# Attention of a two-layer trunk: one pipeline over all groups of tokens and heads, and the largest scores of a head gathered by one product and a DMA

## The chip, the core and the metric

The kernel runs on one core of one Trainium2 chip. A core has five engines with queues of their own: TensorE (PE, whose weight loads are listed apart as PEld), VectorE (DVE), ScalarE (ACT), GpSimd (POOL) and SyncE (SP, which here issues most of the DMAs). PE writes its products into PSUM, from where DVE or ACT take them. The metric is the device time of one execution in microseconds (us). The kernel before took 3489.2 us, the median of 3 runs (3480.62 to 3492.08).

## The reference

A trunk of two layers over 1024 latent tokens and 256 context tokens, with 1024 features. Each layer mixes the tokens in four ways (an mLSTM, an attention, an SSD and an S5 mixer, 256 features each), projects the four results out and then runs a gated feed-forward net. Only the attention is touched:

```python
q = jnp.concatenate([q_nope, q_rope], axis=-1)      # 4 heads, 64 + 32 features
k = jnp.concatenate([k_nope, jnp.broadcast_to(kr, k_nope.shape[:-1] + (MLA_ROPE,))], axis=-1)

def attend(q, k, v):
    s = jnp.einsum('bqhd,bkhd->bhqk', q, k).astype(jnp.float32) * scale
    p = jax.nn.softmax(s, axis=-1).astype(v.dtype)
    return jnp.einsum('bhqk,bkhd->bqhd', p, v)

yc = attend(qc, kc, vc)              # context tokens see the context alone
yl = attend(ql, k_all, v_all)        # latent tokens see all 1280
```

## The kernel before

Tokens lie along the free axis, in ten chunks of 128: chunks 0 and 1 are the context, 2 to 9 the latents. Queries are worked on in groups of columns: (0,256) for the context, (256,512) and (768,512) for the latents. Layer 0 has all three groups and ten chunks; the last layer drops the context's queries and has two groups and eight chunks. To keep single-precision accuracy, queries and keys are each held as a high part (`qh`, `kh`) and a small remainder (`ql`, `kl`), and a product of scores is three matmuls: high by high, high by low, low by high (L1020 to L1022).

**Largest scores.** `scores(h)` (L952) makes the keys of head h, and then the largest score of each query, so that the exponent stays in range. For each chunk of 128 queries it makes one to three products `a_pm` (L970), chunk by 512 or 256 keys, of the high parts alone; DVE reduces each to one column of `a_mx` (L971), and a second small reduce (L972) joins the columns of a chunk. For each group, one product per chunk with that single column as weights and the identity as data (`a_pmr`, L975) lays the chunk's 128 maxima into one row of PSUM, on partition 96; ACT copies the row, negated, into row 96 of `qh` (L976). Row 96 of `kh` holds ones, so the first matmul of a score product, over 97 rows (L1020), subtracts the maximum by itself. A single-precision product of this kind stands in the trace as two matmuls, so 72 products `a_pmr` are 144 records.

**Attention.** `attend` (L978) goes over two pairs of heads, and in each over the heads, the groups and steps of two key chunks (`k0` = 0, 2, ... 8; the context group has one step). One step is six matmuls into `a_pst`, a tile of two PSUM banks of which there is only one; an exponential on ACT into `a_E` (L1024, three buffers); the two value products into `a_po` (L1014, one bank) of the step before; and two sums of the exponentials over the keys into `a_S`, one on POOL and one on DVE (L1033). A group's last value products come right after its last step, then ACT and DVE move `a_po` out (L1036, L1037). `finish` (L1039) closes a group of a pair of heads: a sum on DVE, two products with ones that add `a_S` over the partitions (`a_pr`, L1044), the reciprocal (L1045), the product on POOL (L1046) and the DMA of the result to `YD`. It is put off to a later step by the list `later`; before the pair's next use, `a_S` (one buffer for each group) has to be read by it.

**What sets the order.** `scores(h + 1)` is written before head h's groups, and between groups `extra()` puts in cells of the mLSTM and pieces of the modulation (`wm` loads of 512 KB, products `pm1_...`, L172 and L183) by a fixed table. The program is then ordered on each engine by a list scheduler at build time, which goes by data, buffers and priorities; `TOGETHER` raises that of the value products and of `a_pr`. In this stretch `K.acc` hands out just two PSUM banks in turn (pool `pd`), and key products, `a_pm`, `a_pmr` and `a_pr` all take them in the order in which the program is written. `a_pr` of head 1 is written after all of `scores(3)`, and takes its bank after it.

## Time and profile before

| | us |
|---|---|
| median of 3 runs | 3489.2 (3480.62 to 3492.08) |
| the profiled execution | 3488.96 |
| its span in the profile | 3487.1 |
| PE busy | 3223.8 (92% of the span) |
| DVE busy | 2133.4 (61%) |
| ACT busy | 1217.1 (35%) |
| POOL busy | 1180.6 (34%) |

The profile is of one execution: every instruction of each engine with its start, its duration and what ended the idle time ahead of it. Times inside it count from the span's start. The attention of layer 0 lies from 567 to 864 us, that of layer 1 from 2410 to 2663 us. Busy times of a long stretch say little on what a short one waits for; the stretch itself has to be looked at.

### The profile page before, as it was taken

What the parts mean: (1) busy time and instruction counts of PE and PEld (TensorE: products, weight loads), DVE (VectorE), ACT (ScalarE), POOL (GpSimd) and SP (SyncE); (2) the same over time, 40 slices, a digit from 0 to 9 for tenths busy, and PEclk for the clock granted to TensorE, in tenths of its full rate; (3) what the DMA queues carried; (4) which work ended last, traced back from release to release, by engine and by line L of the source; (5) the groups of instructions that cost most, each with busy time, mean ns of one, the idle gap of its engine ahead of it and who ended that gap; (6) DMA issues with size and microseconds to landing.
All of it is one profiled execution on the core that took longest, in us unless ns stands there. A gap on an engine that the chain in (4) does not pass through costs nothing.

```text
span 3487.1 us, 47319 instructions
## 1 busy us (share of the span) xinstructions
PE 3223.8 (92%) x17678; PEld 2655.9 (76%) x17678; DVE 2133.4 (61%) x4065; ACT 1217.1 (35%) x2025; POOL 1180.6 (34%) x1109
## 2 busy tenths in 40 slices
PE   7899997997989999998999899997988899999996
PEld 6898895554778888886788789995645788887785
DVE  7857648675485343439778583536855855555654
ACT  4223534332244333333211424533323444444211
POOL 1912424223146444442211021323323376554120
PEclk9999997998999999999999999998989999999998
DMA  5677534254322121225332465534152322223321
GB/s 203 168 205 216 161 113 144 92 188 146 133 67 85 65 73 66 73 78 187 116 103 84 126 209 167 154 115 128 53 208 97 103 91 80 83 89 136 127 78 49
DMA packets 287157, 423.51 MB, mean 121 GB/s; under 512 B 91016, under 2 KB 197200, under 8 KB 286928
## 3 DMA queue, kind: packets, MB, share of 16 engines
q1 hardware_dynamic: 176788, 301.29, 27.5%
q10 hardware_dynamic: 110140, 119.20, 10.3%
q8 instruction: 139, 2.28, 0.3%
q14 instruction: 90, 0.74, 0.1%
HBM read 301.48 MB, written 118.91 MB: 121 GB/s over the span
## 4 chain that ended last, share of the span: by engine, by line
PE 38%; DVE 8%; DMA 3%; ACT 2%; issue 2%; POOL 0%; SPq 0%; ACTq 0%; DVEq 0%; POOLq 0%
PE pd L313 4%; PE pd L314 4%; PE pd L312 4%; PE px L312 2%; PE px L314 2%; PE px L313 2%; PE ps_in L312 1%; PE ps_in L314 1%; PE ps_in L313 1%; PE a_po L1014 1%; PE pz L312 1%; PE pz L313 1%; PE pz L314 1%; PE ps_out L312 1%; PE ps_out L313 1%
## 5 line engine op out<-in xcount | busy, mean ns | idle before, releaser
L313 PE MATMUL pd<-fl,wh_d 128*128 128x512 f32 (+1 forms) x896 | 334.0, 376 | 16.3 <-DVE fl L230 16.3
L312 PE MATMUL pd<-fh,wh_d 128*128 128x512 f32 (+1 forms) x896 | 328.6, 377 | 21.4 <-ACT fh L229 10.1
L314 PE MATMUL pd<-fh,wl_d 128*128 128x512 f32 (+1 forms) x896 | 329.6, 373 | 0.0
L230 POOL TENSOR_TENSOR wl_d<-wr_d,wh_d 128x1024 fp32r<-128x1024 f32 x44 | 110.7, 2534 | 472.5 <-ACT wh_d L229 472.4
L1709 DVE SCALAR_TENSOR_TENSOR xx<-pd,modv,xx 128x512 f32<-128x512 f32 (+1 forms) x248 | 165.3, 678 | 122.8 <-PE pd L314 122.0
L312 PE MATMUL ps_in<-ha,wh_in 128*128 128x384 f32 (+3 forms) x688 | 216.7, 325 | 11.8 <-ACT st L1533 11.3
L314 PE MATMUL ps_in<-ha,wl_in 128*128 128x384 f32 (+3 forms) x688 | 222.0, 323 | 0.0
L313 PE MATMUL ps_in<-ha,wh_in 128*128 128x384 f32 (+3 forms) x688 | 221.9, 323 | 0.0
L312 PE MATMUL ps_in<-hc,wh_in 128*128 128x256 f32 (+1 forms) x704 | 214.6, 307 | 7.3 <-ACT hc L244 4.6
L312 PEld LDWEIGHTS pd<-fh,wh_d 128*128 128x128 f32 x896 | 172.1, 193 | 57.5 <-ACT fh L229 12.8
L313 PE MATMUL ps_in<-hc,wh_in 128*128 128x256 f32 (+1 forms) x704 | 214.0, 305 | 0.7 <-DVE hc L245 0.7
L314 PE MATMUL ps_in<-hc,wl_in 128*128 128x256 f32 (+1 forms) x704 | 213.2, 303 | 0.0
L313 PEld LDWEIGHTS pd<-fl,wh_d 128*128 128x128 f32 x896 | 173.0, 194 | 48.3 <-DVE fl L230 21.0
L314 PEld LDWEIGHTS pd<-fh,wl_d 128*128 128x128 f32 x896 | 172.9, 193 | 28.3
L230 POOL TENSOR_TENSOR wlo_u<-wr_u,whi_u 128x1024 fp32r<-128x1024 f32 x44 | 106.0, 2410 | 215.9 <-ACT whi_u L229 194.6
L971 DVE TENSOR_REDUCE a_mx<-a_pm 128x1 f32<-128x512 f32 (+1 forms) x200 | 112.8, 589 | 61.5 <-PE a_pm L970 60.2
L1024 ACT ACTIVATE a_E<-a_pst 128x1024 f32<-128x1024 f32 (+1 forms) x84 | 84.3, 1003 | 186.7 <-PE a_pst L1022 165.7
L229 ACT CAST wh_d<-wr_d 128x1024 fp32r<-128x1024 f32 x44 | 45.2, 1048 | 298.1 <-PE pd L313 213.8
L230 DVE TENSOR_TENSOR wlo_s<-wr_s,whi_s 128x1024 fp32r<-128x1024 f32 x42 | 71.1, 1694 | 119.9 <-ACT whi_s L229 119.9
L312 PEld LDWEIGHTS ps_in<-ha,wh_in 128*128 128x128 f32 x688 | 132.3, 193 | 14.7 <-ACT st L1533 12.0
L312 PEld LDWEIGHTS ps_in<-hc,wh_in 128*128 128x128 f32 x704 | 134.9, 192 | 9.7 <-ACT hc L244 5.6
L313 PEld LDWEIGHTS ps_in<-hc,wh_in 128*128 128x128 f32 x704 | 135.3, 192 | 2.6 <-DVE hc L245 1.9
(647 smaller groups left out, 9496.9 us busy)
## 6 DMA issues: line engine op xcount, KB each, us to landing
wm<-in_w_mod SPq DMA_DIRECT2D x96, 512.0 KB
wr_in<-in_w_in SPq DMA_DIRECT2D x44, 512.0 KB
wr_u<-in_w_up SPq DMA_DIRECT2D x44, 512.0 KB
wr_g<-in_w_up SPq DMA_DIRECT2D x44, 512.0 KB
wr_d<-in_w_down SPq DMA_DIRECT2D x44, 512.0 KB
wr_out<-in_w_out SPq DMA_DIRECT2D x32, 512.0 KB
HD<-u ACTq DMA_DIRECT2D x22, 640.0 KB
hr<-HD SPq DMA_DIRECT2D x22, 640.0 KB
```

Source lines behind the costliest of these rows:

```text
L229: nc.scalar.copy(hi, src)
L230: (eng or nc.gpsimd).tensor_tensor(lo, src, hi.bitcast(F32), OP.subtract)
L312: mm(ps, whi(k), ahi(k), start=start and i == 0, stop=False)
L313: mm(ps, whi(k), alo(k), start=False, stop=False)
L314: mm(ps, wlo(k), ahi(k), start=False, stop=stop and i == len(ks) - 1)
L971: nc.vector.tensor_reduce(mx[:, c, j:j + 1], ps[:, :kw], mybir.AxisListType.X, OP.max)
L1014: nc.tensor.matmul(po[64 * i:64 * i + 64, :w], vt[:, k0 + i, h], E[:, i, :w], start=k0 == 0, stop=k0 + 2 == nk)
L1024: nc.scalar.activation(E[:, :, :w], ps[:, :, :w], AF.Exp, scale=scale)
L1709: nc.vector.scalar_tensor_tensor(v, ps, K.modv[l][:, 8 * part + m, c:c + 1], v, OP.mult, OP.add)
```

## The change

The change rewrites the second half of `scores` and the loop of `attend`.

In `scores`, the largest scores of a chunk stay apart in `mx` (three columns) and are joined for all latent chunks of a head by one reduce into `mf`. One product per head, with the head's 8 or 10 columns of `mf` as weights, lays them as 8 or 10 rows of 128; ACT copies these, negated, into the small tile `row`, and a DMA on SP's queue writes them one behind the other into row 96 of `qh`. The product for each chunk and the copies for each group go.

In `attend`, `old` is carried over groups and heads: the last value products of a group, and moving `po` out, are written inside the first step of the next group. `S` has three parts in place of four: the sum of the pair's first head is joined at once into `S[:, 2]`, so that the second head can use the first two again. `finish` reads `S[:, 2]` and `S[:, 0]`, and what has been put off is done at `k0 == 4`, or in the context's single step.

```diff
@@ -960,20 +960,22 @@
                         lambda k: self.kvh[:, 0, t0:t0 + w], lambda k: self.kvl[:, 0, t0:t0 + w], 1)
             nc.scalar.copy(kh[:64, t0:t0 + w], ps[:64, :w])
             nc.vector.tensor_tensor(kl[:64, t0:t0 + w], ps[:64, :w], kh[:64, t0:t0 + w].bitcast(F32), OP.subtract)
-        mx = pool.tile([P, NCH, 4], F32, tag="mx", name=n(f"mx{h}"), bufs=2)
-        for t0, w in self.groups:
-            cs = range(t0 // P, (t0 + w) // P)
-            for c in cs:
-                ks = [(0, 256)] if c < 2 else [(0, 512), (512, 512), (1024, 256)]
-                for j, (k0, kw) in enumerate(ks):
-                    ps = K.acc(n(f"pm{h}{c}{j}"))
-                    nc.tensor.matmul(ps[:, :kw], qh[:96, c * P:c * P + P], kh[:96, k0:k0 + kw], start=True, stop=True)
-                    nc.vector.tensor_reduce(mx[:, c, j:j + 1], ps[:, :kw], mybir.AxisListType.X, OP.max)
-                nc.vector.tensor_reduce(mx[:, c, 3:4], mx[:, c, :len(ks)], mybir.AxisListType.X, OP.max)
-            ps = K.acc(n(f"pmr{h}{t0}"))
-            for i, c in enumerate(cs):
-                nc.tensor.matmul(ps[96:97, i * P:i * P + P], mx[:, c, 3:4], K.ident, start=i == 0, stop=i == len(cs) - 1, skip_group_check=True)
-            nc.scalar.activation(qh[96:97, t0:t0 + w], ps[96:97, :w], AF.Copy, scale=-1.0)
+        mx = pool.tile([P, NCH, 3], F32, tag="mx", name=n(f"mx{h}"), bufs=2)
+        mf = pool.tile([P, NCH], F32, tag="mf", name=n(f"mf{h}"), bufs=2)
+        c0, m = self.groups[0][0] // P, len(self.oc)
+        for c in oc:
+            ks = [(0, 256)] if c < 2 else [(0, 512), (512, 512), (1024, 256)]
+            for j, (k0, kw) in enumerate(ks):
+                ps = K.acc(n(f"pm{h}{c}{j}"))
+                nc.tensor.matmul(ps[:, :kw], qh[:96, c * P:c * P + P], kh[:96, k0:k0 + kw], start=True, stop=True)
+                nc.vector.tensor_reduce(mf[:, c:c + 1] if c < 2 else mx[:, c, j:j + 1], ps[:, :kw], mybir.AxisListType.X, OP.max)
+        nc.vector.tensor_reduce(mf[:, 2:], mx[:, 2:], mybir.AxisListType.X, OP.max)
+
+        ps = K.acc(n(f"pmr{h}"))
+        nc.tensor.matmul(ps[:m, :P], mf[:, c0:], K.ident, start=True, stop=True)
+        row = pool.tile([NCH, P], F32R, tag="mr", name=n(f"mr{h}"), bufs=2)
+        nc.scalar.activation(row[:m], ps[:m, :P], AF.Copy, scale=-1.0)
+        nc.sync.dma_start(qh.bitcast(F32)[96:97, c0 * P:].rearrange("o (c t) -> o c t", t=P), row.bitcast(F32)[:m])
 
     def attend(self, pool, epool, y_put, extra):
 
@@ -989,30 +991,44 @@
             while later:
                 later.pop(0)()
 
+        def values(po, h, w, nk, k0, E):
+            with K.tc.high_priority(TOGETHER):
+                for i in range(2):
+                    nc.tensor.matmul(po[64 * i:64 * i + 64, :w], vt[:, k0 + i, h], E[:, i, :w], start=k0 == 0, stop=k0 + 2 == nk)
+
+        def finish(h, t0, w, y, r, S):
+            ps = K.acc(n(f"pr{h}{t0}"))
+            nc.vector.tensor_tensor(S[:, 0], S[:, 0], S[:, 1], OP.add)
+            with K.tc.high_priority(TOGETHER):
+                for i in range(2):
+                    nc.tensor.matmul(ps[64 * i:64 * i + 64, :w], K.ones[:, :64], S[:, 2 - 2 * i], start=True, stop=True)
+            nc.vector.reciprocal(r, ps[:, :w])
+            nc.gpsimd.tensor_tensor(y, y, r, OP.mult)
+            y_put(2 + h // 2, 1, y[:, None, :w], t0, w)
+
+        def evac(po, h, w, y, r):
+            me, ot = slice(64 * (h % 2), 64 * (h % 2) + 64), slice(64 - 64 * (h % 2), 128 - 64 * (h % 2))
+            nc.scalar.copy(r[me, :w], po[ot, :w])
+            nc.vector.tensor_tensor(y[me, :w], po[me, :w], r[me, :w], OP.add)
+
+
         self.scores(0, pool)
+        old, ends = None, []
         for hp in range(2):
             ys = {}
             for ho in range(2):
                 h = 2 * hp + ho
                 kh, kl, qh, ql = self.kh[ho], self.kl[ho], self.qh[h], self.ql[h]
-                me, ot = slice(64 * ho, 64 * ho + 64), slice(64 - 64 * ho, 128 - 64 * ho)
                 if h < 3:
                     self.scores(h + 1, pool)
                 for t0, w in groups:
                     extra()
                     if not ho:
                         ys[t0] = [pool.tile([P, w], F32, tag=f"a{i}{t0}", name=n(f"{i}{hp}{t0}")) for i in "yr"]
-                        ys[t0].append(epool.tile([P, 2, 2, w], F32, tag=f"S{t0}", name=n(f"S{hp}{t0}"), bufs=1))
+                        ys[t0].append(epool.tile([P, 3, w], F32, tag=f"S{t0}", name=n(f"S{hp}{t0}"), bufs=1))
                     y, r, S = ys[t0]
-                    po = K.pa.tile([P, 512], F32, tag="m", name=n(f"po{h}{t0}"))
                     nk = 2 if t0 < TC else NCH
-                    old = None
-
-                    def values(k0, E):
-                        with K.tc.high_priority(TOGETHER):
-                          for i in range(2):
-                            nc.tensor.matmul(po[64 * i:64 * i + 64, :w], vt[:, k0 + i, h], E[:, i, :w], start=k0 == 0, stop=k0 + 2 == nk)
-
+                    po = None
                     for k0 in range(0, nk, 2):
                         ps = K.pa.tile([P, 2, 512], F32, tag="s", name=n(f"pst{h}{t0}{k0}"))
                         for i in range(2):
@@ -1024,32 +1040,25 @@
                         nc.scalar.activation(E[:, :, :w], ps[:, :, :w], AF.Exp, scale=scale)
                         if old:
                             values(*old)
-                        if k0 == 2:
-                            settle()
+                            if not k0:
+                                ends.pop(0)()
                         for i in range(2):
                             if nk == 2:
-                                eng[i].tensor_copy(S[:, i, ho], E[:, i, :w])
+                                eng[i].tensor_copy(S[:, i], E[:, i, :w])
                             elif k0:
-                                eng[i].tensor_tensor(S[:, i, ho], old[1][:, i, :w] if k0 == 2 else S[:, i, ho], E[:, i, :w], OP.add)
-                        old = k0, E
-                    values(*old)
-                    nc.scalar.copy(r[me, :w], po[ot, :w])
-                    nc.vector.tensor_tensor(y[me, :w], po[me, :w], r[me, :w], OP.add)
-
-                    def finish(h=h, t0=t0, w=w, y=y, r=r, S=S, hp=hp):
-                        ps = K.acc(n(f"pr{h}{t0}"))
-                        nc.vector.tensor_tensor(S[:, 0], S[:, 0], S[:, 1], OP.add)
-                        with K.tc.high_priority(TOGETHER):
-                          for i in range(2):
-                            nc.tensor.matmul(ps[64 * i:64 * i + 64, :w], K.ones[:, :64], S[:, 0, i], start=True, stop=True)
-                        nc.vector.reciprocal(r, ps[:, :w])
-                        nc.gpsimd.tensor_tensor(y, y, r, OP.mult)
-                        y_put(2 + hp, 1, y[:, None, :w], t0, w)
-
-                    settle()
-                    if ho:
-                        later.append(finish)
+                                eng[i].tensor_tensor(S[:, i], old[5][:, i, :w] if k0 == 2 else S[:, i], E[:, i, :w], OP.add)
+                        if k0 == 4 or nk == 2:
+                            settle()
+                        po = po or K.pa.tile([P, 512], F32, tag="m", name=n(f"po{h}{t0}"))
+                        old = po, h, w, nk, k0, E
+                    ends.append(functools.partial(evac, po, h, w, y, r))
+                    if not ho:
+                        nc.vector.tensor_tensor(S[:, 2], S[:, 0], S[:, 1], OP.add)
+                    else:
+                        later.append(functools.partial(finish, h, t0, w, y, r, S))
                     extra()
+        values(*old)
+        ends.pop(0)()
         settle()
```

Since a scheduler sets the order, the code alone doesn't show where the instructions come to stand. Three places follow, in layer 0, with the order that the build gives.

PE, at the end of the products for head 3's maxima (`a0_pm3..`, two digits of chunk and part behind the head), before: `a0_pr1768` is the sum over partitions for head 1, group 768, `a0_pst27688` the scores of head 2, group 768, step 8, `a0_po2768` its value products, and `pm1_..` modulation.

```order
L970 MATMUL a0_pm380_8453<-a0_kh1_6517,a0_qh3_6600 128x512
L970 MATMUL a0_pm381_8456<-a0_kh1_6517,a0_qh3_6600 128x512
L970 MATMUL a0_pm382_8459<-a0_kh1_6517,a0_qh3_6600 128x256
L970 MATMUL a0_pm390_8463<-a0_kh1_6517,a0_qh3_6600 128x512
L970 MATMUL a0_pm391_8466<-a0_kh1_6517,a0_qh3_6600 128x512
L970 MATMUL a0_pm392_8469<-a0_kh1_6517,a0_qh3_6600 128x256
L975 MATMUL a0_pmr3768_8473<-cst_60,a0_mx3_8374 1x128 x3
L1044 MATMUL a0_pr1768_8498<-a0_S0768_7638,ones_68 64x512 x2
L975 MATMUL a0_pmr3768_8473<-cst_60,a0_mx3_8374 1x128
L172 MATMUL pm1_12_8750<-wm1_12_8745,sc_84 32x512 x8
L1014 MATMUL a0_po2768_8662<-a0_E27686_8705,a0_vt_6520 64x512 x2
L1020 MATMUL a0_pst27688_8711<-a0_qh2_6599,a0_kh0_6516 128x512
```

After, the same place:

```order
L970 MATMUL a0_pm391_8390<-a0_kh1_6517,a0_qh3_6600 128x512
L172 MATMUL pm1_0_8542<-wm1_0_8467,sc_84 32x512 x8
L970 MATMUL a0_pm392_8393<-a0_kh1_6517,a0_qh3_6600 128x256
L183 MATMUL pm1_0_8542<-msel_82,wms1_0_8551 128x2 x4
L975 MATMUL a0_pmr3_8397<-cst_60,a0_mf3_8317 10x128
L1004 MATMUL a0_pr1768_8420<-a0_S0768_7598,ones_68 64x512 x2
L1004 MATMUL a0_pr30_8749<-a0_S10_8404,ones_68 64x256
L172 MATMUL pm1_4_8563<-wm1_4_8558,sc_84 32x512 x8
L183 MATMUL pm1_4_8563<-msel_82,wms1_4_8572 128x2 x4
L1004 MATMUL a0_pr3256_8822<-a0_S1256_8474,ones_68 64x512
L997 MATMUL a0_po2768_8600<-a0_E27686_8634,a0_vt_6520 64x512 x2
L1036 MATMUL a0_pst27688_8640<-a0_qh2_6599,a0_kh0_6516 128x512
```

`a0_pr1768` still comes behind the last product for head 3's maxima, and the first of the two matmuls of the next sums (`a0_pr30`, `a0_pr3256`), which read `S[:, 2]`, now stand here too. Between the last matmul but one of the step ahead (`a0_pst27686`) and `a0_pr1768` there stood 16 products `a0_pm3..` before, and there stand 7 now; in layer 1 it is 14 and 5.

SP, from the loads of modulation weights to the first input tiles of the stage behind the attention, before:

```order
L156 DMA wm1_4_8633<-in_w_mod 128x1024 x4
L156 DMA wm1_8_8654<-in_w_mod 128x1024 x4
L1736 DMA yraw0_4_0_9001<-YD_100 128x256
L1736 DMA yraw0_4_256_9005<-YD_100 128x512
L1736 DMA yraw0_4_768_9009<-YD_100 128x512
L1736 DMA yraw0_5_0_9013<-YD_100 128x256
L1740 DMA x00_8997<-in_x 128x8x256
L1740 DMA x0256_8993<-in_x 128x8x512
L299 DMA wr_out0_0_256_9100<-in_w_out 128x1024
L156 DMA wm1_12_8745<-in_w_mod 128x1024 x4
```

After:

```order
L156 DMA wm1_4_8558<-in_w_mod 128x1024 x4
L156 DMA wm1_8_8579<-in_w_mod 128x1024 x4
L978 DMA a0_qh3_6600<-a0_mr3_8399 1x10x128
L1745 DMA yraw0_4_0_8931<-YD_100 128x256
L1745 DMA yraw0_4_256_8935<-YD_100 128x512
L1745 DMA yraw0_4_768_8939<-YD_100 128x512
L1745 DMA yraw0_5_0_8943<-YD_100 128x256
L156 DMA wm1_12_8671<-in_w_mod 128x1024 x4
```

The DMA that writes head 3's row into `qh` comes to stand right behind the eight loads `wm1_4` and `wm1_8`, and ahead of the first loads of `yraw`.

ACT, before: `a0_E37688` is the last exponential of head 3, `hb...` are casts of the mixers' results for the projection behind the attention.

```order
L1024 ACTIVATE a0_E37688_8919<-a0_pst37688_8912 128x1024
L1036 COPY a0_r1768_8660<-a0_po3768_8856 64x512
L229 CAST hb004_8961<-yraw0_4_0_9001 128x256
L229 CAST hb004_8961<-yraw0_4_256_9005 128x512
L229 CAST hb004_8961<-yraw0_4_768_9009 128x512
L229 CAST hb005_8963<-yraw0_5_0_9013 128x256
L229 CAST hb005_8963<-yraw0_5_256_9017 128x512
```

After, eleven exponentials ahead of the last one: `a0_E27688` is the last of head 2, `a0_E300` the first of head 3.

```order
L1040 ACTIVATE a0_E27688_8647<-a0_pst27688_8640 128x1024
L229 CAST hb004_8891<-yraw0_4_0_8931 128x256
L229 CAST hb004_8891<-yraw0_4_256_8935 128x512
L229 CAST hb004_8891<-yraw0_4_768_8939 128x512
L229 CAST hb005_8893<-yraw0_5_0_8943 128x256
L181 COPY wms1_8_8663<-pm1_8_8654 128x512
L1011 COPY a0_r1768_8585<-a0_po2768_8600 64x512
L1040 ACTIVATE a0_E300_8700<-a0_pst300_8693 128x2x256
```

The casts stood behind all exponentials; now the first four of the 24 stand between those of heads 2 and 3, and eight more further on between the exponentials of head 3. The projection's first products, some 35 of them, have moved into the same stretch on PE.

## Rows read from the trace of the kernel before

**Rows 1.** The page: span and count of instructions.
```profile
span 3487.1 us, 47319 instructions
```
**Rows 2.** Busy time by stretch: us, then PE, PEld, DVE, ACT, POOL, PEclk, DMA share, GB/s.
```profile
586.00:785.00 199.00, 195.20 (x1066) 118.64 (x1067) 141.24 (x330) 69.68 (x103) 48.61 (x45) 0.95 0.39 133
785.00:809.00 24.00, 19.54 (x90) 9.17 (x89) 15.93 (x29) 4.32 (x6) 3.58 (x3) 0.79 0.78 279
...
2429.00:2585.00 156.00, 153.51 (x830) 91.29 (x831) 112.01 (x243) 54.02 (x76) 43.82 (x37) 0.99 0.40 142
2585.00:2606.00 21.00, 13.32 (x40) 5.62 (x38) 15.12 (x24) 2.92 (x4) 3.78 (x3) 0.72 0.25 86
```
**Rows 3.** Timeline 776:812, layer 0: start, us, engine line op, shapes [idle before <-releaser].
```profile
780.52 1.02 ACT L1024 ACTIVATE a_E<-a_pst 128x1024 f32<-128x1024 f32 x1 [2.02 <-PE a_pst L1022]
...
787.64 1.92 PE L172 MATMUL pm<-wm,sc 128*32 128x512 f32 x16
...
791.31 0.82 PE L975 MATMUL a_pmr<-cst,a_mx 128*1 128x128 f32 x6
...
795.36 1.79 DVE L971 TENSOR_REDUCE a_mx<-a_pm 128x1 f32<-128x512 f32 x3
...
804.54 3.36 DVE L1045 RECIPROCAL a_r<-a_pr 128x512 f32<-128x512 f32 x1 [1.89 <-PE a_pr L1044]
804.65 1.27 POOL L1033 TENSOR_TENSOR a_S<-a_E,a_E 128x512 f32<-128x512 f32 x1 [36.98 <-PE a_pr L1044]
...
808.53 1.02 ACT L1024 ACTIVATE a_E<-a_pst 128x1024 f32<-128x1024 f32 x1 [1.56 <-DVE a_S L1033]
```
**Rows 4.** Timeline of ACT, 2578:2612, the same place in layer 1.
```profile
2582.26 1.02 ACT L1024 ACTIVATE a_E<-a_pst 128x1024 f32<-128x1024 f32 x1 [2.42 <-PE a_pst L1022]
2605.30 1.02 ACT L1024 ACTIVATE a_E<-a_pst 128x1024 f32<-128x1024 f32 x1 [3.11 <-DVE a_S L1033]
```
**Rows 5.** Timeline 820:832, last head of layer 0.
```profile
822.45 1.02 ACT L1024 ACTIVATE a_E<-a_pst 128x1024 f32<-128x1024 f32 x1 [1.27 <-PE a_pst L1022]
...
823.52 1.08 PE L1014 MATMUL a_po<-a_E,a_vt 128*64 128x512 f32 x4 [0.58 <-ACT a_E L1024]
...
826.30 1.02 ACT L1024 ACTIVATE a_E<-a_pst 128x1024 f32<-128x1024 f32 x1 [2.83 <-PE a_pst L1022]
```
**Rows 6.** Instructions on tile a_mx, whole span: count, min/median/max ns, first and last start.
```profile
L975 PE MATMUL a_pmr<-cst,a_mx x144: 270/272/421, 585.3 to 2601.3; 128*1 128x128 f32 x144
L972 DVE TENSOR_REDUCE a_mx<-a_mx x72: 135/147/157, 585.1 to 2598.2; 128x1 f32<-128x3 f32 x64, 128x1 f32<-128x1 f32 x8
```
**Rows 7.** Groups by line, 586:785: count, busy us, mean ns, idle before.
```profile
L975 PE MATMUL a_pmr<-cst,a_mx 128*1 128x128 f32 x62 | 10.0, 276 | 0.7 <-DVE a_mx L971 0.7
```
**Rows 8.** Groups by line, 2429:2585.
```profile
L975 PE MATMUL a_pmr<-cst,a_mx 128*1 128x128 f32 x40 | 6.5, 288 | 0.0
```
**Rows 9.** Waits of PEld, 566:880: us in total, times, longest.
```profile
PEld a_pm L970 <- DVE a_mx L971: 7.2, 13, 1.1
```
**Rows 10.** Waits of PEld, 2410:2680.
```profile
PEld a_pm L970 <- DVE a_mx L971: 10.3, 17, 1.2
```
**Rows 11.** Timeline after the last value product of layer 0, 856:882.
```profile
859.84 1.76 ACT L229 CAST hb<-yraw 128x256 fp32r<-128x256 f32 x4
...
860.82 1.01 PE L312 MATMUL ps_out<-hb,wh_out 128*128 128x512 f32 x2 [1.63 <-ACT hb L229]
...
879.63 1.26 PE L312 MATMUL ps_out<-hb,wh_out 128*128 128x256 f32 x5 [2.97 <-ACT hb L229]
```
**Rows 12.** Timeline 582:589: a small load, its reader, and head 0's first score product.
```profile
583.57 0.43 SPq L566 DMA_DIRECT2D xcm<-in_econst  x1
...
585.07 1.02 ACT L570 CAST xlm<-xcm 128x256 bf16<-128x256 f32 x3 [1.64 <-DMA xcm<-in_econst]
...
588.21 0.41 PE L1020 MATMUL a_pst<-a_qh,a_kh 97*128 97x256 f32 x1
```
**Rows 13.** Timeline of SP, 770.5:778: eight loads of 512 KB.
```profile
771.50 5.20 SPq L156 DMA_DIRECT2D wm<-in_w_mod  x8
```


## The prediction

> **What bounds the kernel now.** The page gives the profiled execution's span, 3487.1 us [rows 1]; with the 1.9 us around it that is 3488.96, which lies 0.2 us from the median of the runs, so the sum can be made against it. Some 550 us of the span are attention. The second view is the table of stretches. It splits each layer's attention into a long dense part and a short hole [rows 2]. In the dense parts PE is busy for 195.20 of 199.00 us and for 153.51 of 156.00, while DVE has 141 and 112, ACT 70 and 54. There, PE is full and only a product less shortens the time. In the holes it is the other way round: PE is busy for 19.54 of 24.00 and 13.32 of 21.00 us, and the exponentials stand still.
>
> The third view, the timeline of layer 0's hole, says why [rows 3]. The exponential of head 2's third step starts at 780.52, the next at 808.53. The POOL sum at 804.65, which is of the second step, had waited 36.98 us for `a_pr` (L1044), since its `a_S` was still to be read for head 1. `a_pr` starts only after the last maxima of head 3, because it takes its PSUM bank after theirs. The three buffers of `a_E` then fill up, ACT stops, and PE has just the score products, each of which waits for a DVE reduce to free a bank. Layer 1 has the same hole, from 2582.26 to 2605.30 [rows 4]. Where nothing else is left to do, one step follows the last after 826.30 − 822.45 = 3.85 us [rows 5].
>
> **The change part by part.**
>
> *A, products that go.* All maxima take 144 records on L975 and 72 small reduces on L972 [rows 6]. Of these, 62 records lie in layer 0's dense part and 40 in layer 1's [rows 7, 8]. Their busy time overlaps with their neighbours', so I price one by a run of them: six in 0.82 us, which is 0.137 us [rows 3]. That makes 102 × 0.137 = 14.0 us of a full PE. The eight new products are 16 records of as many columns; at 0.137 us, 16 × 0.137 = 2.2 us, of which the dense parts get some three quarters, 1.6. A is −12. It ends at 0, if PE then waits for something else as long, and at −20, the busy time of both rows (16.5 us) and some weight loads.
>
> *F, fewer small reduces between the big ones.* PE's weight loads wait 7.2 and 10.3 us for the big reduces to free a bank [rows 9, 10], 17.5 us in all. The 72 small ones, of 147 ns, go from DVE: 10.6 us that stood ahead of big ones. Not all of these lay in a wait, so I take half of the 17.5, −9; the ends are 0 and −25, the waits and part of the 10.6.
>
> *B, the hole.* `a_pr` of head 1 still comes behind the last product for head 3. But where the step before is done there were 16 such products left (14 in layer 1), and now there are 7 (5). In the hole they go at the pace of DVE's reduces, three in 1.79 us or 0.60 us each [rows 3]. Nine fewer in each layer is 2 × 9 × 0.60 = 10.8, B = −11. The products themselves are not saved; they move into the dense part, where PE ran other work, and where the waits of F show that they can be had more cheaply. The ends: 0, if the 5.4 us a layer come back there, and −43, if both holes shrink to one step (28.0 + 23.0 − 2 × 3.9).
>
> *C, behind layer 0's attention.* Before, the four casts that follow the last value products took 1.76 us, 0.44 each, and PE waited 1.63 and 2.97 us for such casts [rows 11]. Twelve casts (5.3 us of ACT) now stand among the exponentials of head 3, and some 35 products of the output projection stand there on PE, where a step of 3.85 us holds products for about 2.7 (1.65 of scores, 1.06 of values [rows 5]). The waits alone are 4.6; 35 products at 1.26 / 5 = 0.25 us are 8.8 [rows 11]. I take the middle, −7; the ends are 0, if casts of late `yraw` hold up the exponentials behind them, and −10.
>
> *The pipeline over groups* takes no work away. A group's last value products and its moving out come under the next group's first exponential; in dense parts that gap was already filled by other products, so I cost it at nothing there. In the tail, where nothing fills it, it is part of C.
>
> *D, the DMA of the row.* The step from ACT's copy to the first score product now has a DMA in it. Nearest is a small load: issued at 583.57, read at 585.07, 1.5 us [rows 12]. Behind each head's transposing product stand nine key products and pieces of the cells, which PE can run meanwhile; behind the waiting score product everything else on PE stands still. I take half of the 1.5 uncovered, 0.7 a head, for seven of the eight heads: 5 us. The eighth, head 3 of layer 0, is issued on SP right behind eight loads of 512 KB. Before, those took SP 5.20 us to issue [rows 13], and their first product on PE started at 787.64 [rows 3], 16.1 us after 771.50. The row is only needed after the last step of head 2, so I take a quarter, 4. D = +9; the ends are 0 and 7 × 1.5 + 16.1 = 27.
>
> The Trainium skill ("DMA: Bandwidth & Descriptors", section "Anatomy of one DMA — SWDGE (gpsimd) path") has a fixed cost of about 2.0 us for a DMA, mostly the receipt of the write. It speaks of GpSimd's path, and the trace's 1.5 us on SP's is below it. By the 2.0, wholly uncovered for seven heads, D would be +18 and the time 9 us longer, an estimate from that page.
>
> *E, a later start.* Head 0's first score product stood at 588.21 [rows 12], behind the maxima of the context's two chunks. Now it needs those of all chunks: 24 products more in layer 0, 12 in layer 1. At 0.60 us these are 14.4 + 7.2 = 21.6. They have to run in any order, and PE is what is full; only ACT and POOL start later. I take a fifth, +4, with ends at 0 and +18 (of the 21.6, what key products and cells don't cover).
>
> The sum: −12 − 9 − 11 − 7 + 9 + 4 = −26, so 3488.96 − 26 = 3463. Its own range, with the terms partly set against each other, is 3440 to 3480.
>
> **The rivals.**
>
> *R1, hidden anyway: 3488.* PE's dense parts may be held up by DVE's big reduces and by the cells as much as by PE's own load; then A and F give nothing, as each product that goes is a longer wait for the next bank. B gives 5, C 7, and D and E take 13: about 1 less than before. For it: the waits of F. Against it: 98% of PE's time in those stretches is busy [rows 2]. Chance 0.15.
>
> *R2, slower: 3506.* The row's DMA stands on SP, which issues in order and may itself be waiting, or be busy with loads, when the row is ready. If each of seven heads meets a batch such as the eight loads, which kept SP for 5.20 us [rows 13], and head 3 of layer 0 the whole 16.1, D is 7 × 5.2 + 16.1 = 52.5. With the rest at −35, that is +17.5, or 3506. It decides from D = 35: with 4 for head 3 of layer 0, from 31 / 7 = 4.4 us for each other head. For it: the row stands behind `wm1_4` and `wm1_8` in the new order, and score products on PE wait for it with all that comes behind them. Against it: the small load had 1.5 us, and SP's loads are spread through the stretch. Chance 0.17.
>
> The same page ("Queues, rings and completion order") says that descriptors are consumed in ring order on each DMA engine, with one ring of SP's on each. By that a small row can't pass the loads issued ahead of it on SP, which speaks for R2 at head 3; no row here shows a small DMA behind such loads.
>
> *R3, more than forecast: 3429.* If the holes shrink to a few us, since the sums on POOL and DVE are read earlier and `a_pr` is no longer the last thing, B is −30 (of at most 43); with A 14, F 17, C 10, and +11 for D and E, that is −60. For it: both holes hang on one late product. Against it: that product still comes behind all of head 3's maxima. Chance 0.18.
>
> **How the numbers follow.** The forecast has 0.50. About 0.3%, ±10.5 us, is what can be told from no change: 3478.5 to 3499.4. Faster takes all of R3, 0.45 of the forecast's 0.50 (its range ends just beyond the bound) and 0.03 of R1: 0.66. The same takes 0.04 of the forecast, 0.11 of R1 and 0.01 of R2: 0.16. Slower takes the rest, 0.18: 0.16 of R2, and 0.01 each of the forecast and R1, with the unknown costs at their upper ends. The range reaches from just below R3 to short of R2: 3425 to 3495, which leaves R2 out.
>
> **What would show it.** A: PE's dense parts shorter at the same busy share, 16 records for the maxima in place of 144. F: the weight loads' waits for `a_mx` at half. B: holes around the late `a_pr` of some 22 and 17 us. C: casts among head 3's exponentials, and no waits of 1.6 and 3 us for casts behind the attention. D: the first score product of a head, with the row's DMA as its releaser and less than 1 us of idle; more than 4 there would be R2. E: head 0's first exponentials some 10 us later with PE busy. The prediction is wrong if the dense parts don't shorten, if the holes stay or go, or if PE stands at a head's first score product.

## The result, and the profile after

The changed kernel takes 3447.8 us, the median of 4 runs (3445.2 to 3458.1), against 3487.5 for the kernel before: ratio 0.9893, 95% interval 0.9867 to 0.9920. That is 37 us less (1.1%), where 26 had been forecast; 3448 lies inside the range of 3425 to 3495, and inside the likeliest case's own, 3440 to 3480.

The page of the profile after:

```profile
span 3443.4 us, 47008 instructions
```

The span is 43.7 us shorter than in [rows 1]. Of that, 41.1 lie in the two attentions. To have like against like, I cut both traces at the same two instructions: a layer's first key product (`a_pkn`) and a fixed product of the projection behind the attention (`ps_out`, third weight block, token group 256). The view of stretches, cut there; columns as in [rows 2], layer 0 and then layer 1. Before:

```profile
567.20:894.10 326.90, 293.17 (x1476) 174.80 (x1477) 215.61 (x435) 113.48 (x178) 99.28 (x87) 0.90 0.44 151
2402.70:2667.50 264.80, 238.35 (x1120) 138.10 (x1120) 175.93 (x336) 91.12 (x128) 81.28 (x60) 0.91 0.37 128
```

After:

```profile
567.70:860.70 293.00, 271.82 (x1404) 167.63 (x1405) 214.26 (x405) 106.93 (x169) 100.94 (x87) 0.94 0.48 168
2362.90:2620.50 257.60, 229.61 (x1054) 133.61 (x1054) 166.50 (x306) 85.19 (x121) 74.98 (x57) 0.92 0.37 127
```

Three numbers come out of each stretch. *Idle* is the stretch less PE's busy time: 326.9 − 293.2 = 33.7. *Lost to the clock* is half of the time in which PE was busy at the lower of the two levels that the clock's records know, 2.4 and 1.2 GHz. In layer 0 before, the lower level stood for 64.5 us of the stretch (a PEclk of 0.90); laid over PE's busy times, the records show PE busy in 57.0 of them, so 28.5 us are lost. In the other 7.5 us PE was idle, which is counted already. *Work* is what is left of the busy time, 264.7. The last row of the table is a second execution of the changed kernel's order, from the first experiment below.

| us, both layers | stretches | idle | lost to the clock | work |
|---|---|---|---|---|
| before | 591.7 | 60.2 | 49.3 | 482.2 |
| after | 550.6 | 49.2 | 35.3 | 466.1 |
| difference | −41.1 | −11.0 | −14.0 | −16.1 |
| the same order again, difference to before | −37.1 | −11.0 | −7.7 | −18.4 |

All three parts fell. Idle time repeats from one execution of the order to the other; the clock's part does not (14.0 and 7.7 us), and the work's does within 2.3. Some 2 us of the work are ten products of the projection that come behind the cut in layer 1's new order (10 × 0.23 us). The clock is a part that the forecast did not have. Layer 0 gave 33.9 of the 41.1, layer 1 just 7.2. By stage, with times from the traces (from the first key product to the first score product; to the exponential ahead of the hole; the hole; to the last exponential; to the projection's product):

| us | start | dense | hole | tail | behind | sum |
|---|---|---|---|---|---|---|
| layer 0 before | 21.0 | 192.3 | 28.0 | 48.5 | 37.1 | 326.9 |
| layer 0 after | 45.2 | 150.4 | 20.9 | 54.6 | 21.8 | 293.0 |
| layer 1 before | 27.2 | 152.4 | 23.0 | 47.5 | 14.7 | 264.8 |
| layer 1 after | 42.4 | 143.1 | 15.2 | 50.4 | 6.6 | 257.6 |

The stretches of [rows 2] in the profile after:

```profile
612.90:763.40 150.50, 149.77 (x827) 95.35 (x826) 115.25 (x250) 53.87 (x80) 48.66 (x43) 1.00 0.34 117
763.40:784.30 20.90, 18.85 (x130) 9.22 (x129) 13.75 (x29) 3.96 (x8) 4.76 (x5) 1.00 0.77 289
2405.20:2548.30 143.10, 137.35 (x709) 80.94 (x708) 100.72 (x197) 47.46 (x66) 41.77 (x33) 0.98 0.38 138
2548.30:2563.50 15.20, 11.47 (x50) 4.59 (x48) 9.89 (x14) 2.83 (x5) 3.10 (x3) 0.89 0.49 173
```

Layer 0's dense part now has PE busy for all but 0.7 us, at the full clock. The hole of layer 0 (the second row) is hardly one for PE: 18.85 of 20.90 us busy at 1.00, against 19.54 of 24.00 at 0.79 in [rows 2]. The timeline of that place, as in [rows 3]:

```profile
763.38 1.02 ACT L1040 ACTIVATE a_E<-a_pst 128x1024 f32<-128x1024 f32 x1 [2.29 <-PE a_pst L1038]
...
778.83 0.39 PE L975 MATMUL a_pmr<-cst,a_mf 128*10 128x128 f32 x2
...
779.14 1.50 PE L1004 MATMUL a_pr<-a_S,ones 128*64 128x512 f32 x6
...
780.31 1.26 POOL L1049 TENSOR_TENSOR a_S<-a_E,a_E 128x512 f32<-128x512 f32 x1 [10.38 <-PE a_pr L1004]
...
784.26 1.02 ACT L1040 ACTIVATE a_E<-a_pst 128x1024 f32<-128x1024 f32 x1 [0.25 <-DVE a_S L1049]
```

The same chain holds the exponential up (maxima, `a_pr`, sum on POOL). The sum on POOL starts 16.9 us after the exponential ahead of the hole, where it was 24.1 before. (The two waits, 10.38 and 36.98 us, can't be compared: POOL did a piece of a cell at 769.32 in between.) The tile `a_mf`, as in [rows 6]:

```profile
L975 PE MATMUL a_pmr<-cst,a_mf x16: 272/277/359, 610.1 to 2557.2; 128*10 128x128 f32 x8, 128*8 128x128 f32 x8
...
L972 DVE TENSOR_REDUCE a_mf<-a_mx x8: 162/172/178, 609.9 to 2556.8; 128x8 f32<-128x24 f32 x8
```

16 records for 144, 8 small reduces for 72. Where head 0 of layer 0 starts, the row's DMA on SP and the product that waits for it:

```profile
610.84 0.87 SPq L978 DMA_DIRECT2D a_qh<-a_mr  x1
...
612.90 0.19 PEld L1036 LDWEIGHTS a_pst<-a_qh,a_kh 97*128 97x128 f32 x1 [0.22 <-DMA a_qh<-a_mr]
```

From issue to use it is 2.06 us, with 0.22 of them uncovered; that is the only wait on this DMA that the table of waits has, in either layer. The row of head 3 in layer 0, behind the eight loads, and the first product that reads it:

```profile
773.13 5.87 SPq L156 DMA_DIRECT2D wm<-in_w_mod  x8
779.54 0.78 SPq L978 DMA_DIRECT2D a_qh<-a_mr  x1
```

```profile
791.38 0.38 PE L1036 MATMUL a_pst<-a_qh,a_kh 97*128 97x256 f32 x1
```

In the trace's DMA packets, this row's ten of 512 bytes go 5.8 to 7.5 us after its issue, when the loads' packets end. Six other rows have theirs 1.3 to 1.6 us after. So this row did wait behind the loads, but it had 11.8 us until it was read.

### The profile page after: what moved, and what is told of

It reads as the page before. It is cut to its first block, busy times and chain, and to the rows that moved or that the text cites. A ratio compares the mean times of both kernels' runs of the same rounds, so it can differ in the third digit from the quotient of the medians.

```text
span 3443.4 us, 47008 instructions
## 1 busy us (share of the span) xinstructions
PE 3191.5 (93%) x17550; PEld 2644.8 (77%) x17550; DVE 2128.9 (62%) x4011; ACT 1207.4 (35%) x2013; POOL 1177.6 (34%) x1109
## 5 line engine op out<-in xcount | busy, mean ns | idle before, releaser
L312 PE MATMUL pd<-fh,wh_d 128*128 128x512 f32 (+1 forms) x896 | 328.8, 377 | 21.9 <-ACT fh L229 12.8
L229 ACT CAST wh_d<-wr_d 128x1024 fp32r<-128x1024 f32 x44 | 45.2, 1047 | 289.9 <-PE pd L313 157.2
L312 PEld LDWEIGHTS ps_in<-ha,wh_in 128*128 128x128 f32 x688 | 132.8, 194 | 14.9 <-ACT st L1542 11.8
```

Source lines behind the costliest of these rows:

```text
L229: nc.scalar.copy(hi, src)
L312: mm(ps, whi(k), ahi(k), start=start and i == 0, stop=False)
```

## The experiments

Each was timed in 5 rounds beside the kernel before; all changes are against the changed kernel unless the text says otherwise. All the stretches are cut at the two instructions named above, and all ledgers are worked out as there.

**The pipeline taken out again.**

```diff
-                    po = None
+                    po, old = None, None
...
-                    ends.append(functools.partial(evac, po, h, w, y, r))
+                    values(*old)
+                    evac(po, h, w, y, r)
```

> The change without its pipeline over groups: each group's last value products and its moving out are written at the group's own end again, as before; the rest (one product and one DMA per head, S in three parts, settling at k0 == 4) stays. The built order of every engine is the same as that of the whole change. Theory 1 (the scheduler had already filled that gap, the pipeline is worth nothing): 3448 us, within 0.3% of the whole change. Rival (the pipeline is part of the gain): 3458 or more, a fourth of the 40 us lost.

3447.9 us, ratio 0.9889 (0.9871 to 0.9907): the same as with it. Written group by group or as one pipeline, the list scheduler builds the same order for all five engines. The part of the change that its name speaks of is worth nothing here. Since the order is the same, its profile is a second execution of the changed kernel's order:

```profile
574.20:869.20 295.00, 273.91 (x1396) 168.62 (x1406) 213.92 (x406) 107.08 (x169) 101.04 (x87) 0.92 0.49 167
2370.00:2629.60 259.60, 231.45 (x1046) 134.49 (x1054) 168.06 (x306) 86.22 (x122) 75.44 (x58) 0.90 0.37 127
```

Each stretch is 2.0 us longer than in the changed kernel's profile. Idle time is the same within 0.2 us, and the clock loses 3.5 and 2.8 more. Smaller differences of one stretch, in what follows, are not told from chance.

**The new `attend` alone**, with the old `scores`.

> The new attend with the old scores: the maxima are gathered with one product per chunk and ACT copies per group, as before. Theory 1 (most of the gain is in the maxima: 144 records and 72 small reduces gone, and fewer products ahead of the late a_pr): only the casts and projection products beside head 3 remain, some 9 us, and 13 products for head 3's maxima ahead of a_pr in place of 16 and 14, 2 us: 3476, ratio to before 0.997. Theory 2 (most of the gain is what the smaller S lets happen behind the attention): 20 us or more, 3465 or less, ratio 0.994 or less.

3481.0 us, ratio 0.9986 (0.9976 to 0.9995). Of the 37 us, some 5 come without the new gathering and 32 with it, which is theory 1; it had 11 for what remains.

```profile
569.40:883.50 314.10, 285.45 (x1467) 168.68 (x1478) 218.32 (x440) 112.64 (x177) 101.37 (x87) 0.94 0.46 157
2388.60:2657.50 268.90, 242.25 (x1103) 138.17 (x1110) 169.40 (x335) 90.08 (x126) 74.85 (x58) 0.89 0.36 123
```

Layer 0 is 12.8 us shorter than before and layer 1 4.1 longer. In layer 0, tail and what is behind fall from 48.5 + 37.1 to 51.6 + 24.2, by 9.8: that is C. The holes are longer, 32.9 and 27.1, although 13 products for head 3's maxima stand ahead of `a_pr` in place of 16 and 14: their count alone does not set a hole's length.

**`a_pr` from another pool**, in the changed kernel and in the kernel before:

```diff
-            ps = K.acc(n(f"pr{h}{t0}"))
+            ps = K.pb.tile([P, 512], F32, tag="m", name=n(f"pr{h}{t0}"))
```

> The kernel before with the same single edit: a_pr takes its bank from pb. Theory 1: the holes of 28.0 and 23.0 us shrink to a step, 43 us at most, of which 30 products for the maxima at 0.60 us and modulation come back in the dense parts: 3465, ratio 0.993. Rival (the hole is no loss): 3485 to 3490. If it comes near 3448, the hole is as large a lever as the whole change.

> The whole change, but a_pr takes its PSUM bank from the pool of three (pb, which cells and modulation use here) and no longer queues behind the maxima in pd. In the order a_pr of head 1 now stands ahead of the step that waited. Theory 1 (the holes of 20.9 and 15.2 us hang on that bank): exponentials of that step follow each other in less than 8 us in both layers, and some 28 us of hole go, of which the products that ran in them (12 at 0.60 us and modulation) come back: 3428, ratio to the kernel before 0.983. Rival (PE's work just moves, the hole is no loss): 3445 to 3450.

The kernel before with this line alone: 3451.8 us, ratio 0.9909 (0.9895 to 0.9922), −32 by the ratio, nearly the whole gain of the change. The changed kernel with it: 3442.6, ratio 0.9885 (0.9869 to 0.9902), which the intervals don't tell from the change alone. Stretches, the kernel before with the line first:

```profile
571.10:879.70 308.60, 281.75 (x1467) 171.44 (x1478) 214.82 (x435) 113.25 (x178) 99.29 (x87) 0.92 0.46 160
2386.50:2637.20 250.70, 233.12 (x1112) 136.99 (x1119) 175.40 (x336) 91.07 (x128) 81.19 (x60) 0.94 0.38 135
```

```profile
571.30:868.30 297.00, 271.89 (x1396) 166.87 (x1406) 208.80 (x404) 106.77 (x169) 99.87 (x87) 0.94 0.48 166
2369.30:2617.10 247.80, 222.07 (x1047) 129.85 (x1054) 164.69 (x306) 85.74 (x121) 75.13 (x57) 0.96 0.38 132
```

Both holes are one step in both (3.9 and 4.0; 4.0 and 5.1 us). In the kernel before, that is worth 15.8 us of idle and 15.4 of clock, 32.4 in all with its work lower by 1.2. In the changed kernel the clock gives 9.4 and idle and work take 3.6 back. Layer 0 even takes 4.0 us more: PE had been at work through its hole. The expected 3428 took the length of a hole for its cost. The two edits don't add up, because in part they take away the same loss: in the stretches, the line alone gives 32.4 us, the change alone 41.1, and both together 46.9.

**Gathering group by group** (20 products and DMAs, not 8), alone and with `a_pr` from `pb`:

```diff
-        for c in oc:
+        for t0, w in self.groups:
+            c0, m = t0 // P, w // P
+            for c in range(c0, c0 + m):
...
-        nc.tensor.matmul(ps[:m, :P], mf[:, c0:], K.ident, start=True, stop=True)
+            nc.tensor.matmul(ps[:m, :P], mf[:, c0:c0 + m], K.ident, start=True, stop=True)
```

> The whole change, but the maxima are gathered group by group: one product and one DMA for each group of a head (20 of each) in place of one for each head (8). Head 0 can start as early as before; in the order, 14 and 13 products for head 3's maxima stand ahead of the late a_pr again (7 and 5 in the whole change). Theory 1 (what the gather gains is a shorter hole): the holes are 27 us or more again and the gain mostly goes: 3465 to 3475. Rival (the 128 records less and the 72 small reduces less are the gain, as the forecast's A and F had it): 3448 or less, since both still go and the late start of head 0 goes too.

> Gathering group by group, and a_pr from the pool pb. The hole is gone by the order, head 0 starts early, and products for head 3's maxima may run beside its own first steps, where PE waits for ACT. Theory 1 (with the hole gone, one product per head costs the late start and the idle tail, some 5 us a layer): 3433. Rival (the start and the tail don't matter): 3442, as with one product per head.

3460.0 (0.9919, 0.9904 to 0.9933) and 3454.3 (0.9908, 0.9895 to 0.9921). The first lies between the two expectations: the holes are back at 27.2 and 22.9 us, and a quarter of the gain goes by the ratio, a third by the medians, not most of it; the interval just overlaps that of the changed kernel. The second met neither: with the hole at that step gone, gathering by groups is 12 us slower by the medians and 8 by the ratio than gathering once, with intervals that just overlap, though I had it 10 faster. Stretches of the first, then of the second:

```profile
568.80:875.80 307.00, 279.84 (x1420) 166.75 (x1421) 217.29 (x408) 108.02 (x177) 99.32 (x87) 0.92 0.47 160
2379.50:2634.40 254.90, 227.67 (x1062) 130.51 (x1062) 169.47 (x310) 86.81 (x125) 73.22 (x57) 0.93 0.38 128
```

```profile
567.90:868.80 300.90, 273.71 (x1421) 165.86 (x1422) 212.12 (x410) 108.25 (x177) 100.20 (x87) 0.94 0.48 165
2372.70:2626.50 253.80, 230.51 (x1061) 133.05 (x1061) 163.40 (x310) 86.16 (x125) 75.26 (x57) 0.92 0.37 129
```

Against gathering once with `a_pr` from `pb`, the stretches are 9.9 us longer: idle is within 0.3 us, the work is 2.8 more and the clock loses 7.4 more, all of that in layer 1. The exponentials now stand still at another step, 20.0 us from 729.56 and 19.8 from 2537.47, where the longest such times with gathering once are 11.2 and 12.4. Why the clock is lower in layer 1 wasn't settled.

**The old products put back for nobody** (144 records into tiles that nothing reads):

```diff
+            if c % 4 == 1 or c == 9:
+                cs = [q for q in oc if (q + 2) // 4 == (c + 2) // 4]
+                ps = K.acc(n(f"pmd{h}{c}"))
+                for i, q in enumerate(cs):
+                    nc.tensor.matmul(ps[96:97, i * P:i * P + P], (mf[:, q:q + 1] if q < 2 else mx[:, q, 0:1]), K.ident, ...)
```

> The whole change, with the old products of one column added back (144 records into PSUM tiles that nobody reads, in the places where they stood, each group's tile from pool pd); the small reduces and ACT copies stay away. The forecast's A (0.137 us a record on a full PE): 144 x 0.137 = 20 us, 3468. Theory 1 (PE has slack beside DVE's reduces; the records cost little, the wait in the hole is what counts: 10 and 6 products ahead of a_pr in place of 7 and 5): 3 x 0.6 + 1 x 0.6 and a quarter of the records, 5 to 8 us: 3455.

3480.0 us, ratio 0.9975 (0.9964 to 0.9986): 32 us longer, which takes most of the gain back.

```profile
569.10:889.30 320.20, 292.50 (x1485) 173.29 (x1486) 209.89 (x404) 107.43 (x169) 99.89 (x87) 0.92 0.44 153
2394.10:2656.90 262.80, 236.88 (x1117) 135.79 (x1117) 168.72 (x307) 86.37 (x122) 73.39 (x58) 0.92 0.36 126
```

Against the changed kernel the work is 21.3 us more, 0.148 a record, near the forecast's price of 0.137; 4.4 of idle and 6.7 of clock come with it (32.4 in all). Theory 1 as I had put it, that the records cost little, fell. They cost their time, and half as much again comes on top; the holes are 29.0 and 17.9 us. That it is the banks which they take that hold up other work wasn't tried by itself. The small reduces were put back in no run by themselves.

**The room that the smaller `S` left, taken up again:**

```diff
+        pad = epool.tile([P, 1024], F32, name=n("pad"))
```

> The whole change with 4 KB of each partition taken up again by a tile that nobody uses, beside the sums S. In the order, no cast stands among the exponentials any more (0 of 24 for layer 0, 12 in the whole change). Theory (the casts and projection products moved because the smaller S left room for their tiles, and that is worth what the loop alone showed in layer 0): 9 us longer, 3457. Rival (the move gives nothing, or another cause of it): 3446 to 3450.

3467.3 us, ratio 0.9935 (0.9920 to 0.9949).

```profile
566.20:881.40 315.20, 275.82 (x1405) 168.82 (x1406) 208.44 (x405) 107.86 (x169) 98.74 (x87) 0.92 0.46 157
2384.80:2635.30 250.50, 223.36 (x1053) 129.60 (x1053) 164.40 (x306) 85.13 (x121) 76.77 (x57) 0.94 0.38 131
```

Layer 0 is 22.2 us longer, layer 1 7.1 shorter. In layer 0, tail and behind are 50.9 + 36.8 in place of 54.6 + 21.8, 11.3 more: the casts moved because of room, and are worth some 10 us there. The other 11 are in the start and the dense part, which the tile changed too; so 3467 is no clean price of the casts.

**More PSUM banks for the maxima:**

```diff
-                ps = K.acc(n(f"pm{h}{c}{j}"))
+                ps = K.pb.tile([P, 512], F32, tag="m", name=n(f"pm{h}{c}{j}")) if j == 1 else K.acc(n(f"pm{h}{c}{j}"))
```

> The whole change, with the second of the three products for a chunk's maxima taking its bank from the pool pb, so that DVE's reduces have more banks to work from. In the order, the last maxima of head 3 and the late a_pr stand ahead of the step that waited in layer 1, and close behind it in layer 0. Theory (PE's waits for reduces and the hole cost idle time and, with it, time at the lower granted clock): the holes are under 8 us, idle and half-clock time in both attentions are below those of the whole change (49 and 78 us): 3438 or less. Rival (DVE's reduces set the pace whatever the banks): 3446 or more.

3475.7 us, ratio 0.9976 (0.9962 to 0.9989), slower than either expectation, with the holes at 12.6 and 5.3 us. The stretch from the first key product to the first score product, in the changed kernel and here:

```profile
567.70:612.90 45.20, 36.42 (x143) 24.21 (x143) 35.44 (x78) 15.24 (x34) 8.63 (x13) 0.67 0.46 158
```

```profile
568.70:651.70 83.00, 60.82 (x243) 40.57 (x245) 50.35 (x121) 19.88 (x42) 15.22 (x21) 0.63 0.40 132
```

A hundred products more, most of them of mLSTM cells, run ahead of the first score product, with 22.2 us of idle and 24.7 lost to the clock in this one stretch (8.8 and 13.5 in the changed kernel). The late start that the forecast priced at 4 us is costly when it grows. Why the order came out so wasn't tried.

**Head 0 alone by groups**, and **the row's DMA from ACT**. The first takes the code of gathering by groups with

```diff
+        gs = self.groups if h == 0 else [(self.groups[0][0], T - self.groups[0][0])]
```

and the second is

```diff
-        nc.sync.dma_start(qh.bitcast(F32)[96:97, ...
+        nc.scalar.dma_start(qh.bitcast(F32)[96:97, ...
```

> The whole change, but head 0 alone gathers its maxima group by group (3 products and DMAs in layer 0, 2 in layer 1), so that its first score product can start some 20 us earlier; the other heads gather once. The forecast's E (a late start costs a fifth of the 24 + 12 products): 4 us less, 3444. Theory (PE ran 82 more matmuls ahead of the first score product in layer 0, with only 1.2 us more of idle time, so the late start costs nothing): 3448, within 0.15%.

> The whole change with the row's DMA issued by ACT, not SP, so that it stands behind no load. The forecast's D (9 us, 4 of them behind the eight loads): 4 to 9 us less, 3439 to 3444. Theory (the trace has PE idle for 0.36 us or less ahead of each head's first score product but one, so the row is hidden on either queue): 3448, within 0.15%; ACT's issue takes its time, some 0.5 us a head at most.

3444.9 (0.9888, 0.9869 to 0.9906) and 3439.6 (0.9871, 0.9851 to 0.9892). Neither is told from the changed kernel by its interval. Stretches, head 0 first:

```profile
570.90:861.30 290.40, 268.09 (x1399) 164.12 (x1410) 215.13 (x405) 106.81 (x171) 97.33 (x87) 0.95 0.48 169
2365.50:2620.70 255.20, 228.80 (x1049) 131.61 (x1055) 169.99 (x308) 87.00 (x123) 75.36 (x57) 0.92 0.38 130
```

```profile
568.40:862.10 293.70, 272.55 (x1395) 168.45 (x1405) 214.81 (x404) 107.02 (x169) 100.85 (x87) 0.93 0.49 168
2363.50:2614.20 250.70, 222.77 (x1046) 129.51 (x1053) 164.62 (x306) 85.13 (x121) 76.81 (x57) 0.95 0.38 131
```

Head 0 early takes 2.6 and 2.4 us off the stretches, hardly more than the 2.0 each by which two executions of one order differ, so E is not told from nothing. The row on ACT's queue leaves layer 0, where the eight loads stand ahead of it, at 293.7 us (293.0 with SP), so no wait went there. Layer 1 is 6.9 shorter, 6.3 of it clock. But the kernel with the padding tile, whose rows stay on SP, has 250.5 us in layer 1 too: its built order of PE there is the same as with ACT's queue, and unlike the changed kernel's. So those 7 us go with an order, not with the queue.

**The best of two layers put together**: head 0 by groups in layer 0, `a_pr` from `pb` in layer 1.

> The whole change with the two best stretches of the runs put together: in layer 0, head 0 gathers its maxima group by group (its attention took 290.4 us there, from the first key product to a fixed product of the projection, against 293.1 for the whole change), and in layer 1 a_pr takes its bank from pb (247.7 against 257.6). The built order of PE in layer 0 is that of the first of these, and in layer 1 nearly that of the second. Theory (idle time and time at the lower clock come with an order, so they can be put together): 3448 - 2.7 - 9.9 = 3435, ratio to before 0.985. Rival (the layers' differences are chance from one execution to the next): 3445, ratio 0.988.

3440.7 us, ratio 0.9864 (0.9843 to 0.9885), the lowest ratio of all.

```profile
571.90:863.30 291.40, 268.45 (x1399) 164.25 (x1410) 213.98 (x405) 106.83 (x171) 97.76 (x87) 0.95 0.49 169
2371.70:2619.20 247.50, 221.77 (x1046) 129.70 (x1053) 164.25 (x306) 85.58 (x121) 75.17 (x57) 0.96 0.38 132
```

Both stretches came out within 1.0 us of the expected ones (290.4 and 247.7), with idle and clock within 0.6 us. Here an order's idle and clock came again with it, but in the first experiment the clock differed by up to 3.5 us. The whole did not reach 3435: what lies outside the two stretches took 2903.3 us in this profile, 2892.8 in the changed kernel's and 2896.2 in that of the first experiment. Against the changed kernel it is 7 us less by the medians, and the intervals overlap, so it isn't told from it.

## Why the prediction was right, and where it wasn't

The direction and the range held, and the sum was off by 11 to 15 us (−26 against −37 by the ratio and −37 to −41 in the stretches). The terms met it unevenly, and errors of both signs stand against each other.

- **A, −12: right in mechanism, a little short.** It counted the records of the dense parts, 102 less 12; the stretches have 128 fewer. The work fell by 16.1 us, some 2 of it for the products behind the cut, and the 144 records put back cost 0.148 us of work each.
- **F, −9: wrong.** The waits for the big reduces did not halve. The table of waits of the weight loads has, in layer 0 (566 to 880 us) and in layer 1 (2362 to 2680 us):

```profile
PEld a_pm L970 <- DVE a_mx L971: 5.9, 9, 1.1
```

```profile
PEld a_pm L970 <- DVE a_mx L971: 10.4, 15, 1.6
```

  against 7.2 and 10.3 in [rows 9, 10]. PE waits there for the big reduces, of which there are as many as before.
- **B, −11: right in mechanism, short in size.** The holes shrank by 7.1 and 7.8 us, not 5.4 each. But a hole's length is not its cost: taking away what is left of layer 0's gained nothing in the changed kernel.
- **C, −7: right in mechanism**, −9.2 in layer 0 by tail and behind (−9.8 with `attend` alone). The cause is the smaller `S`, as the padding showed; the prediction hadn't said it. Layer 1 gave another 5.2 in the same two stages, which had no term; some 2 of that are the ten products behind the cut.
- **The pipeline, nothing: right**, for the strongest reason there is: the order is the same.
- **D, +9: wrong.** 0.22 us were uncovered. The key products and cells behind each transposing product hide the DMA whole. Head 3's row in layer 0, issued at 779.54, waited behind the loads, but was not asked for until head 2's last step was done, at 791.38.
- **E, +4: not told apart from nothing** by head 0's early start (3444.9 us against 3447.8). A start later by another 38 us, in the kernel with more banks, is dear.
- **The term that is missing: the clock.** It gave 7.7 to 14.0 us of the gain. In both executions the two holes lost some 7 us less (PE was busy there at the lower level for 17.8 us before, for 3.4 and 4.3 after) and the dense parts some 7 less; the later start lost 11 more, and what follows the holes 11 and 5 less. It stood in [rows 2]: PEclk 0.79 and 0.72 in the holes. I read those rows for PE's busy share, and priced the holes by counts of products at the pace of reduces.

So the sum came near in part by luck. Without the 13 us of D and E, and without the 9 of F, it would be −30, and what was missing in A, in the holes, at the end of layer 1 and in the clock is the rest.

R1 fell with A and B; its sum has a slip, since −5 − 7 + 13 is 1 us more than before, 3490 and not 3488. R2 fell with D: one row met a queue on SP, and PE did not wait for it. R3 was further off, on the other side (−60 against −41), and not right in the way: neither hole shrank to a step.

The Trainium skill ("DMA: Bandwidth & Descriptors", section "Anatomy of one DMA — SWDGE (gpsimd) path") gave about 2.0 us for a DMA on GpSimd's path. The row's 2.06 us on SP's queue agree with that better than the 1.5 that I took from a load. It changed nothing, since the time is covered.

## What to carry to other kernels

Before pricing a stall by what is queued in it, make the ledger of the stretch: idle time, time lost while PE is busy at a lower granted clock, and work. Time at the lower clock in which PE is idle costs nothing more. The holes here cost twice, in short waits and in the clock, and two edits that cure the same stretch don't add up. Take a second execution of the same order before a difference of a few us is given a cause. Where a list scheduler sets the order, compare the built orders first: code written as a pipeline may give the same one, and a few KB of room may give another.

## What the runs showed of the hardware

PE's granted clock cost nearly as much as the waits in a stretch where PE counted as busy for 90% of the time: in layer 0 before, 28.5 of 326.9 us were lost to the lower level, with 33.7 of idle time in short waits. Right behind the hole before, score products of 512 columns took 0.80 and 0.63 us each at the lower level, against 0.40 at the full clock in the kernel after (third line):

```profile
811.51 0.80 PE L1020 MATMUL a_pst<-a_qh,a_kh 97*128 97x512 f32 x1
812.11 0.63 PE L1021 MATMUL a_pst<-a_ql,a_kh 96*128 96x512 f32 x1
```

```profile
787.26 0.40 PE L1037 MATMUL a_pst<-a_ql,a_kh 96*128 96x512 f32 x1
```

Over the kernels whose stretches are shown here, the work in layer 0's stays between 254 and 268 us, while idle and clock together go from 34 to 62. That is where orders differ most. A small DMA from SBUF to SBUF took 2.06 us from its issue on SP to its first reader; another one, issued behind eight loads of 512 KB on the same queue, had its packets moved 5.8 to 7.5 us after its issue, in place of 1.3 to 1.6.
